# An encoder trunk on one core: sixteen more chunks of the MLP's activated branch computed with tokens on partitions, and the MLP ordered in groups of 512 columns

## The chip, the core and the metric

The kernel runs on one core of a Trainium2 chip. A core has a matrix engine (TensorE, PE in the profile, with its weight loads as PEld), VectorE (DVE), ScalarE (ACT), GpSimd (POOL) and SyncE (SP), which here issues nearly all DMA transfers. Each engine works through its own queue in order, and engines wait for each other by semaphores. The metric is the device time of one execution in microseconds (us); smaller is better.

## What is computed

Two layers (DEPTH = 2) on 256 tokens of width 1024, all in float32. In each layer a token mixer (pooling, windowed attention, gates) and then a gated MLP with a convolution over tokens on one branch:

```python
def _conv_ffn(xn, w_up, conv_w, conv_b, w_down):
    a, gval = jnp.split(xn @ w_up, 2, axis=-1)
    a = lax.conv_general_dilated(a, conv_w[:, None, :], window_strides=(1,),
                                 padding=((CONV_WIDTH // 2, CONV_WIDTH // 2),), ...)  + conv_b
    return (jax.nn.gelu(a) * gval) @ w_down

def reference(...):
    h = x
    for layer in range(DEPTH):
        h = h + _token_mixer(_rmsnorm(h, norm1[layer]), ...)
        h = h + _conv_ffn(_rmsnorm(h, norm2[layer]), ...)
    return _rmsnorm(h, norm_f)
```

The MLP's inner width D_FF is 2816: 22 chunks of 128 channels. `a` is called the activated branch here and `gval` the gate branch. The convolution has three taps over neighbouring tokens, for each channel by itself.

## The kernel before

**Precision by splitting.** Every float32 operand of a large product is split into a high part in a reduced format that TensorE takes at full pace (`wh`, made by a cast on ScalarE, line 201) and the rest (`wl`, a subtraction on VectorE, line 203). A product is high x high + high x low + low x high. The activations (`x2`, the chunks `act`) are split in the same way.

**Weights** (class `Weights`, line 97). All loads and pieces are listed in order of use (`W.use`, lines 303 to 322 for the MLP). A load is 1 MB, in one of RAW = 3 buffers, and is split as two pieces of 128 x 1024; BUFS = 5 split pieces are held, and `get` (line 224) splits up to LOOK = 3 pieces ahead of the one that is used. Three hooks tie the order: `queue_behind` (line 152) puts the next splits behind given instructions on ScalarE and VectorE, `loads_behind` (lines 135, 722) puts a load behind another DMA in SyncE's queue, and `after_splits` (line 230) puts an instruction behind the latest splits. A scheduler then fixes the order of instructions on each engine when the program is built; nothing is reordered between engines' queues later.

**Two ways to compute a piece of the up projection.**
- `proj` (line 551) with channels on partitions: the weights are the stationary operand. A chunk of 128 channels takes 8 matmuls of 512 columns (high weights against high and low x of 256 tokens) and 8 of 256 columns (low weights against high x). The two sums are added by ScalarE and VectorE (`add_up`, lines 579 and 580).
- `by_tokens` (line 672) with tokens on partitions: x is the stationary operand and 512 columns of weights stream (`v_sum`, line 661). Four chunks take 2 x 4 x 6 = 48 matmuls of 512 columns. The result has to be turned into channels on partitions: `cross` (line 704) does a 32 x 32 block transposition on VectorE (line 711), a write to DRAM (line 713) and four reads from it (line 718), 0.5 MB each way. `by_halves` (line 1245) does a group of four chunks in two halves.

**The MLP before** (lines 1208 to 1333). The gate branch of chunks 0 to 19 is made by tokens, in NQ = 5 groups of four; the activated branch by tokens for chunks 0 to 3 alone, and by `proj`, two chunks at a time, for 4 to 21. `up(f)` (line 1261) finishes a chunk: scaled copy with bias on ScalarE (line 1273), the other two taps on VectorE (lines 1274 and 1277), gelu on ScalarE (1286), the product with the gate branch on VectorE (1288, or 1294 for chunks 20 and 21), then the split into `actq` (ScalarE, 1297) and `actk` (VectorE, 1298). `down` is a generator over the chunks of the down projection (`residual_mm`, line 589): 12 matmuls of 512 columns a chunk (lines 585 to 587); the last four chunks are held and added quarter by quarter of the output (two token halves x two column halves), so that the norm that follows (`Norm.add`, line 441, `to_channels`, line 463) begins while later quarters are still summed. Two chunks are made, and the down projection follows LAG = 6 chunks behind; `HALF_GROUPS` says where the halves of gate groups 3 and 4 stand between them.

**The start of the MLP.** `to_channels` turns the normed tokens to channels: TensorE transposes (line 481), ScalarE makes the high part of `x2` (line 484) and VectorE the low part (line 485), for one half of the tokens (t = 0) and then the other. Behind t = 1, `queue_behind` puts the next six splits behind these parts (lines 489 and 490). The first matmuls by tokens on the new x stand in line 667.

## Time and profile before

| what | value |
|---|---|
| median of 3 runs | 862.62 us (862.19 to 862.68) |
| profiled execution | 862.26 us |
| its span, first to last instruction | 860.5 us |
| granted TensorE clock, mean | 0.999 |
| matmuls | 4343 |
| DMA moved | 186.80 MB, mean 217 GB/s |

The span is what the trace covers; the time of the execution has 1.8 us more around it. Busy times of the engines overlap, so their sum means nothing; an engine's idle time costs only where the chain of work that ended last passes through it. A matmul's end in the trace is modelled: in a stream of matmuls the next one starts before the shown end of the last, so lengths of a stretch are taken from start to start. ScalarE's and VectorE's instructions overlap a little in the same way when they follow each other without a wait.

### The profile page before, as it was taken

The numbers are of one execution on the slowest core, as the hardware profiler recorded it, in microseconds if no ns is written. First come the engines' busy times: TensorE is split into PE (matmuls) and PEld (weight loads), VectorE is DVE, ScalarE is ACT, GpSimd is POOL, SyncE is SP. The second block draws the span as 40 slices with busy tenths as digits, with TensorE's granted clock in tenths as the row PEclk, the third lists the DMA queues.
The fourth block names the chain that finished last, engine by engine and source line by source line (L and its number), as shares of the span: only waits on it lengthen the run. The fifth ranks groups of instructions, "written<-read, shape, count | busy, mean of one in ns | idle before, by whom it ended". The sixth has DMA issues, their size and how long they took to land.

```text
span 860.5 us, 11694 instructions
## 1 busy us (share of the span) xinstructions
PE 852.6 (99%) x4343; PEld 728.3 (85%) x4343; DVE 618.8 (72%) x946; ACT 492.8 (57%) x770; POOL 32.7 (4%) x98
## 2 busy tenths in 40 slices
PE   9999999999999999999999999999999999999997
PEld 8888888888888888888888889888888888888886
DVE  7998786557766787777755987764666766876774
ACT  7656665555445566566545666664554555755662
POOL 1800000000010000000000000000000100000001
PEclk9999999999999999999999999999999999999999
DMA  9686556776747786566626565657876387775741
GB/s 335 210 254 200 196 177 227 240 265 197 256 157 247 269 276 236 196 237 203 244 98 200 187 202 195 207 182 250 274 238 246 131 274 237 267 256 182 243 147 49
DMA packets 136384, 186.80 MB, mean 217 GB/s; under 512 B 5560, under 2 KB 88192, under 8 KB 136328
## 3 DMA queue, kind: packets, MB, share of 16 engines
q1 hardware_dynamic: 136168, 185.79, 64.4%
q8 instruction: 34, 0.56, 0.3%
q10 hardware_dynamic: 160, 0.27, 0.1%
q14 instruction: 22, 0.18, 0.1%
HBM read 172.39 MB, written 13.65 MB: 216 GB/s over the span
## 4 chain that ended last, share of the span: by engine, by line
PE 95%; DVE 2%; ACT 1%; issue 1%; DMA 1%; POOL 0%; POOLq 0%; ACTq 0%
PE proj_ps L543 33%; PE t_ps L667 30%; PE v_ps L667 6%; PE res_ps L587 5%; PE res_ps L585 5%; PE res_ps L586 5%; PE v_ps L895 3%; PE v_ps L802 1%; PE pool_ps L543 1%; PE o_ps L1083 1%; PE s_ps L1034 1%; PE s_ps L1029 1%; PE o_ps L1079 1%; DVE h L445 1%; DMA raw<-in_w_in_dram 1%
## 5 line engine op out<-in xcount | busy, mean ns | idle before, releaser
L203 DVE TENSOR_TENSOR wl<-raw,wh 128x1024 fp32r<-128x1024 f32 x274 | 331.9, 1220 | 134.8 <-ACT wh L201 109.0
L201 ACT CAST wh<-raw 128x1024 fp32r<-128x1024 f32 x274 | 284.9, 1050 | 132.4 <-PE t_ps L667 64.7
L543 PE MATMUL proj_ps<-x,wh 128*128 128x512 f32 x832 | 196.9, 390 | 0.0
L543 PEld LDWEIGHTS proj_ps<-x,wh 128*128 128x128 f32 x832 | 154.3, 188 | 30.9
L667 PE MATMUL t_ps<-wh,x 128*128 128x512 f32 x576 | 180.1, 390 | 0.0
L667 PEld LDWEIGHTS t_ps<-wh,x 128*128 128x128 f32 x576 | 108.2, 188 | 22.4
L667 PE MATMUL t_ps<-wl,x 128*128 128x512 f32 x288 | 112.0, 389 | 0.0
L543 PEld LDWEIGHTS proj_ps<-x,wl 128*128 128x128 f32 x832 | 105.4, 191 | 3.0
L543 PE MATMUL proj_ps<-x,wl 128*128 128x256 f32 x832 | 107.8, 283 | 0.0
L586 PE MATMUL res_ps<-wl,actq 128*128 128x512 f32 (+1 forms) x184 | 69.9, 380 | 0.0
L587 PE MATMUL res_ps<-wh,actk 128*128 128x512 f32 (+1 forms) x184 | 69.9, 380 | 0.0
L585 PE MATMUL res_ps<-wh,actq 128*128 128x512 f32 (+1 forms) x184 | 69.7, 381 | 0.0
L667 PEld LDWEIGHTS t_ps<-wl,x 128*128 128x128 f32 x288 | 54.1, 188 | 11.1
L667 PE MATMUL t_ps<-wh,po 128*128 128x512 f32 x128 | 41.4, 395 | 0.0
L587 PEld LDWEIGHTS res_ps<-wh,actk 128*128 128x128 f32 x184 | 34.6, 188 | 6.6
L586 PEld LDWEIGHTS res_ps<-wl,actq 128*128 128x128 f32 x184 | 34.6, 188 | 6.4
L585 PEld LDWEIGHTS res_ps<-wh,actq 128*128 128x128 f32 x184 | 34.5, 188 | 6.3
L579 ACT COPY a<-proj_ps 128x256 f32<-128x256 f32 x36 | 13.8, 388 | 37.4 <-PE proj_ps L543 37.4
L580 DVE TENSOR_TENSOR a<-proj_ps,a 128x256 f32<-128x256 f32 x36 | 15.0, 423 | 24.5 <-ACT a L579 24.4
L454 POOL TENSOR_SCALAR ss<-ss 128x1 f32<-128x1 f32 x8 | 1.9, 236 | 781.8 <-ACT junk L447 781.8
L667 PEld LDWEIGHTS t_ps<-wh,po 128*128 128x128 f32 x128 | 24.0, 188 | 4.9
L447 ACT ACTIVATE junk<-h 128x512 f32<-128x512 f32 (+1 forms) x19 | 10.5, 554 | 29.6 <-DVE h L445 29.5
(204 smaller groups left out, 1101.0 us busy)
## 6 DMA issues: line engine op xcount, KB each, us to landing
raw<-in_w_in_dram SPq DMA_DIRECT2D x58, 1024.0 KB, 5.8
raw<-in_w_up_dram SPq DMA_DIRECT2D x44, 1024.0 KB, 6.1
raw<-in_w_down_dram SPq DMA_DIRECT2D x22, 1024.0 KB, 4.9
raw<-in_w_a_dram SPq DMA_DIRECT2D x8, 1024.0 KB
raw<-in_w_o_dram SPq DMA_DIRECT2D x8, 1024.0 KB, 7.1
crossing<-crossing SPq DMA_DIRECT2D x12, 512.0 KB, 5.1
turning<-turning SPq DMA_DIRECT2D x8, 512.0 KB, 2.7
turned_p<-turning SPq DMA_DIRECT2D x32, 128.0 KB, 3.3
```

Of the source, the lines that this page charges most:

```text
L201: inst = nc.scalar.copy(out=h, in_=src)
L203: inst = nc.vector.tensor_sub(out=l, in0=src, in1=h.bitcast(F32))
L445: nc.vector.tensor_add(out=h[:, t, cc], in0=ps, in1=h[:, t, cc])
L447: nc.scalar.activation(junk[:, 0 : cc.stop - cc.start], h[:, t, cc], AF.Square, scale=D**-0.5, accum_out=ss[:, n : n + 1],)
L543: nc.tensor.matmul(out, w(k), x, start=(steps is first and k == 0), stop=(steps is last and k == nk - 1), skip_group_check=turns["rest"],)
L579: nc.scalar.copy(out=out, in_=sums[1])
L580: nc.vector.tensor_add(out=out, in0=sums[0], in1=out)
L585: nc.tensor.matmul(ps, ah, wh, start=first, stop=False, skip_group_check=on)
L586: nc.tensor.matmul(ps, ah, wl, start=False, stop=False, skip_group_check=on)
L587: nc.tensor.matmul(ps, al, wh, start=False, stop=last, skip_group_check=on)
L667: nc.tensor.matmul(ps, x2[:, 2 * n + j, part, t, :], w[:, j, :], start=(n + m == 0), stop=(n == last and m == 5),)
L895: nc.tensor.matmul(ps[t], a[:, k, t, :], w[:, j, :], start=(k + m == 0), stop=(k == KD - 1 and m == 2),)
```

## The change

The activated branch of chunks 4 to 19 is made by tokens too, in groups of four, so that only chunks 20 and 21 are left to `proj`. The order is now a list of steps: the activated half (`a`), the gate half (`g`) and the four chunks of the down projection (`d`) of the group before; at the end chunks 20 and 21 by `proj` (`p`) and the down projection of chunks 16 to 21. `CHUNKS_BEHIND` says which chunks `up` finishes behind which half step. Each group has its own half of two buffers for the turned results. In `to_channels`, the next two splits are also put behind the low part of x of token half 0.

```diff
-LAG = 6
-HALF_GROUPS = {4: (3, 0), 8: (3, 1), 12: (4, 0), 14: (4, 1)}
+def _mlp_steps():
+    steps = []
+    for n in range(1, NQ):
+        steps += [("a", n), ("g", n), ("d", 4 * n - 4)]
+    last = 4 * NQ
+    steps.append(("p", last))
+    return steps + [("d", f) for f in (last - 4, last)]
+MLP_STEPS = _mlp_steps()
+CHUNKS_BEHIND = {
+    ("a", 1): ((), (0, 1)), ("g", 1): ((2, 3), ()),
+    **{("d", 4 * n): ((), (4 * n + 4,)) for n in range(NQ - 1)},
+    **{("a", n): ((4 * n - 3,), (4 * n - 2,)) for n in range(2, NQ)},
+    **{("g", n): ((4 * n - 1,), ()) for n in range(2, NQ)},
+    ("p", 4 * NQ): ((4 * NQ - 3, 4 * NQ - 2), (4 * NQ - 1,)),
+}
...
-            if t == 1:
-                W.queue_behind(last, 6)
+            W.queue_behind(last if t else last[1:], 6 if t else 2)
...
-        z_of = [zg[:, 0], zg[:, 1], zga[:, 0]]
-        za = zga[:, 1]
+        z_of = {(kind, n): z[:, n % 2] for kind, z in (("g", zg), ("a", zga)) for n in range(NQ)}
...
-            if f < 4:
+            if f < 4 * NQ:
                 nc.scalar.copy(
-                    out=a.rearrange("p (a j t) -> p t a j", t=2, j=32), in_=of_chunk(za, f)
+                    out=a.rearrange("p (a j t) -> p t a j", t=2, j=32),
+                    in_=of_chunk(z_of["a", f // 4], f % 4),
                 )
             else:
                 sums = proj(x2, 2)
...
+        def half_steps(kind, n):
+            if kind == "p":
+                for f in (n, n + 1):
+                    up(f)
+                    yield
+            elif kind == "d":
+                for _ in range(n, min(n + 4, NF), 2):
+                    next(down)
+                    next(down)
+                    yield
+            else:
+                yield from by_halves(kind, n)
+        for at in MLP_STEPS:
+            if at[0] == "d" and at[1] == 4 * NQ:
+                break
+            chunks = CHUNKS_BEHIND.get(at, ((), ()))
+            for _, some in zip(half_steps(*at), chunks):
+                for f in some:
+                    up(f)
```

The list of loads (lines 303 to 322) follows the same steps: two loads for each `a` and each `g` (512 rows x 512 columns each), two for each `d` of four chunks, and two of 256 columns for `p`.

More of the change, by code (lines that the diff above doesn't have):

```diff
@@ L306, in encoder @@
             W.use(rows(w_up[l], j * 512, 4, 0, 512, tag), slots[2 * j : 2 * j + 2])
-        for n in range(3):
-            for j in range(2):
-                W.use(rows(w_up[l], j * 512, 4, DFF + n * 512, 512))
-        for f in range(4, NF, 2):
-            if f in HALF_GROUPS:
-                n, j = HALF_GROUPS[f]
-                W.use(rows(w_up[l], j * 512, 4, DFF + n * 512, 512))
-            a = cols(w_up[l], f * P)
-            if f >= 4 * NQ:
-                g = cols(w_up[l], DFF + f * P)
-                a = [a[0], g[0], a[1], g[1]]
-            W.use(a)
-            if f >= LAG:
-                W.use(rows(w_down[l], (f - LAG) * P))
-        for f in range(NF - LAG, NF, 2):
-            W.use(rows(w_down[l], f * P))
+        for j in range(2):
+            W.use(rows(w_up[l], j * 512, 4, DFF, 512))
+        for kind, n in MLP_STEPS:
+            if kind == "p":
+                (a0, a1), (g0, g1) = (cols(w_up[l], c + n * P) for c in (0, DFF))
+                W.use([a0, g0, a1, g1])
+            elif kind == "d":
+                for f in range(n, min(n + 4, NF), 2):
+                    W.use(rows(w_down[l], f * P))
+            else:
+                for j in range(2):
+                    W.use(rows(w_up[l], j * 512, 4, (kind == "g") * DFF + n * 512, 512))
     h = const.tile([P, 2, D], F32, name="h")
@@ L1243, in of_chunk, with by_halves @@
             return z[:, :, i].rearrange("p (t a) j -> p t a j", t=2)
-        def by_halves(n):
+        def by_halves(kind, n):
             ps = by_tokens(x2, 4, end=2)
@@ L1248, in by_halves @@
             by_tokens(x2, 4, ps=ps, begin=2)
-            to_z(ps, z_of[n % 3], 0, W.last[1])
+            to_z(ps, z_of[kind, n], 0, W.last[1])
             yield
@@ L1257, in encoder @@
             W.free(i)
-        to_z((ps0, ps1), za, 2, W.behind[1])
-        run(by_halves(0))
+        to_z((ps0, ps1), z_of["a", 0], 2, W.behind[1])
+        run(by_halves("g", 0))
         def up(f):
@@ L1290, in up @@
                     in0=y2.rearrange("p (a j t) -> p t a j", t=2, j=32),
-                    in1=of_chunk(z_of[f // 4 % 3], f % 4),
+                    in1=of_chunk(z_of["g", f // 4], f % 4),
                 )
@@ L1315, in encoder @@
         )
-        for n in (1, 2):
-            for j, _ in enumerate(by_halves(n)):
-                up(2 * (n - 1) + j)
-        groups = {n: by_halves(n) for n in range(3, NQ)}
-        for f in range(4, NF, 2):
-            if f in HALF_GROUPS:
-                next(groups[HALF_GROUPS[f][0]])
-            up(f)
-            up(f + 1)
-            if f >= LAG:
-                next(down)
-                next(down)
+        def half_steps(kind, n):
+            if kind == "p":
+                for f in (n, n + 1):
+                    up(f)
+                    yield
+            elif kind == "d":
+                for _ in range(n, min(n + 4, NF), 2):
+                    next(down)
+                    next(down)
+                    yield
+            else:
+                yield from by_halves(kind, n)
[6 more added lines that the diff above has]
+                    up(f)
         if l + 1 < DEPTH:
```

## The prediction

> **What bounds the kernel now.** I read the page first (span, busy shares, chain), then TensorE's timeline through the MLP, then the timelines of the other engines where the MLP ends, then the DMA issues. From the page:

> ```profile
> span 860.5 us, 11694 instructions
> ...
> PE 852.6 (99%) x4343; PEld 728.3 (85%) x4343; DVE 618.8 (72%) x946; ACT 492.8 (57%) x770; POOL 32.7 (4%) x98
> ...
> PE 95%; DVE 2%; ACT 1%; issue 1%; DMA 1%; POOL 0%; POOLq 0%; ACTq 0%
> ```

> TensorE is busy all the time and makes 95% of the chain that ends last. So nothing on another engine is worth anything here except where it makes TensorE wait, and a change can gain only by cheaper matmuls or by removing one of the few waits. It can lose wherever VectorE (72%) or ScalarE (57%) falls behind for a stretch.

> **The matmuls.** These rows of TensorE's timeline (start, length, line, operation, tiles, shape, count) hold two pairs of chunks by `proj`, 24 matmuls of the down projection, and half a group by tokens:

> ```profile
> 331.01 2.08 PE L543 MATMUL proj_ps<-x,wl 128*128 128x256 f32 x16
> ...
> 332.92 3.82 PE L543 MATMUL proj_ps<-x,wh 128*128 128x512 f32 x16
> ...
> 336.58 0.39 PE L585 MATMUL res_ps<-wh,actq 128*128 128x512 f32 x1
> ...
> 342.02 0.39 PE L667 MATMUL t_ps<-wh,x 128*128 128x512 f32 x1
> ...
> 347.46 3.79 PE L543 MATMUL proj_ps<-x,wh 128*128 128x512 f32 x16
> ...
> 351.08 2.08 PE L543 MATMUL proj_ps<-x,wl 128*128 128x256 f32 x16
> ...
> 353.00 0.40 PE L585 MATMUL res_ps<-wh,actq 128*128 128x512 f32 x1
> ```

> A pair by `proj` took 336.58 - 331.01 = 5.57 us, then 353.00 - 347.46 = 5.54. By tokens the same two chunks are 24 matmuls of 512 columns: 347.46 - 342.02 = 5.44. Both ways stream as many columns; by tokens saves the surplus of the 16 narrow ones, which start 0.12 us apart instead of half of 0.227. The change moves 8 pairs in each of 2 layers: 16 x 0.115 = **1.85 us gained**.

> [...]

> **The x parts.** The other edit puts the next two splits behind the low part of x for token half 0. Before (a group row, then the timeline of VectorE and TensorE at the first layer's start of the MLP):

> ```profile
> L667 PE MATMUL v_ps<-v,x 128*128 128x512 f32 x24 | 7.1, 416 | 0.8 <-DVE x L485 0.8
> ```

> ```profile
> 246.55 1.22 DVE L203 TENSOR_TENSOR wl<-raw,wh 128x1024 fp32r<-128x1024 f32 x1
> ...
> 247.33 0.71 PE L667 MATMUL v_ps<-v,x 128*128 128x512 f32 x2
> ...
> 247.69 0.69 DVE L485 TENSOR_TENSOR x<-xt_ps,x 128x512 fp32r<-128x512 f32 x1
> ...
> 248.43 1.20 PE L667 MATMUL v_ps<-v,x 128*128 128x512 f32 x4 [0.39 <-DVE x L485]
> ```

> A weight's low part (1.22 us) stands ahead of x's, and TensorE waits; the group row holds both layers' waits, 0.8. Since a matmul in a stream starts 0.39 - 0.227 = 0.16 before the modelled end of the last, each costs 0.55: **1.1 us gained**. In the order as built, x's low part now stands ahead of that split, which can start at about 249 and is wanted after 252, so nothing replaces the wait.

> **Work of the other engines.** Per moved chunk VectorE loses an add and gets half a transpose:

> ```profile
> L580 DVE TENSOR_TENSOR a<-proj_ps,a 128x256 f32<-128x256 f32 x36 | 15.0, 423 | 24.5 <-ACT a L579 24.4
> L711 DVE STREAM_TRANSPOSE crossing<-t_ps 128x512 f32<-128x512 f32 x20 | 13.4, 701 | 3.9 <-PE t_ps L667 3.9
> ```

> 32 x 0.423 = 13.5 us go, 16 x 0.701 = 11.2 come; ScalarE copies from SBUF where it copied from PSUM. Hidden under TensorE either way: nothing, until VectorE is what TensorE waits for.

> **A group in the middle.** One cycle (4 activated, 4 gate, 4 down pieces) is 12 x 2.72 = 32.6 us of TensorE; VectorE needs 12 x 1.14 for low parts, 4 x 0.70 for transposes, 4 x 1.46 for chunks: 22.3 us. The chunks of a group are made some 15 us after its gate half and wanted after 32.6. The first weight load behind the crossing is the tightest:

> ```profile
> 293.70 0.37 SPq L713 DMA_DIRECT2D crossing<-crossing  x1
> ...
> 299.93 1.81 SPq L718 DMA_DIRECT2D zga<-crossing  x4
> 301.84 0.94 SPq L137 DMA_DIRECT2D raw<-in_w_up_dram  x2
> ```

> ```profile
> raw<-in_w_in_dram SPq DMA_DIRECT2D x58, 1024.0 KB, 5.8
> raw<-in_w_up_dram SPq DMA_DIRECT2D x44, 1024.0 KB, 6.1
> ```

> SyncE's queue holds the load until the crossing's write has landed and the four reads are issued: 8.1 us, after 1.3 of transposes; 6.1 to land, 2.1 to split: 17.6 us after the gate half. TensorE wants it 8 pieces, 21.8 us, after. 4 us of cover: cost 0. The down projection's loads now come in fours behind a group's gate half instead of in ones; they are as many, and 8 of the 22 loads of w_up in each layer change from runs of 256 columns to runs of 512. I cost that at nothing for the same cover; if it is gone, it is the rival of late crossings.

> **The end of each MLP** is where I expect the loss. Before:

> ```profile
> 396.93 3.79 PE L543 MATMUL proj_ps<-x,wh 128*128 128x512 f32 x16
> ...
> 404.38 3.82 PE L543 MATMUL proj_ps<-x,wh 128*128 128x512 f32 x16
> ...
> 408.04 0.39 PE L585 MATMUL res_ps<-wh,actq 128*128 128x512 f32 x1
> ```

> ```profile
> 403.25 0.42 DVE L580 TENSOR_TENSOR g<-proj_ps,g 128x256 f32<-128x256 f32 x1
> ...
> 413.19 0.42 DVE L1298 TENSOR_TENSOR actk<-g,actq 128x256 fp32r<-128x256 f32 x1
> ```

> The last pairs (chunks 20, 21) take 408.04 - 396.93 = 11.1 us; VectorE starts on their sums 6.3 us after the start and has the last low part at 413.6, with four down pieces (10.9 us) still between 408.04 and the chunks that are held. No wait. After the change only chunks 16 and 17 (5.44 us) lie between, and chunks 17, 18, 19 are made in the same stretch as 20 and 21. In the order as built, VectorE's first sum of the pair (it waits for TensorE, 6.1 us after the pair's start) has 31 instructions behind it up to the low part of chunk 19: in all 7 low parts of weights, 10 passes of the convolution, 15 of 256 columns. Back to back they take less than their length:

> ```profile
> 288.95 3.50 DVE L203 TENSOR_TENSOR wl<-raw,wh 128x1024 fp32r<-128x1024 f32 x3 [0.53 <-ACT wh L201]
> ...
> 283.63 0.87 DVE L1274 SCALAR_TENSOR_TENSOR y<-a,prm,y 128x255 f32<-128x255 f32 x2
> ...
> 285.21 0.75 DVE L1288 TENSOR_TENSOR g<-y,zg 128x256 f32<-128x256 f32 x2
> ```

> ```profile
> 287.88 3.90 ACT L201 CAST wh<-raw 128x1024 fp32r<-128x1024 f32 x4
> ...
> 269.86 1.08 ACT L1273 ACTIVATE y<-a,prm 128x256 f32<-128x256 f32 x2
> ```

> Spacings: (3.50 - 1.22)/2 = 1.14, 0.39, 0.33. So 7 x 1.14 + 10 x 0.39 + 15 x 0.33 = 16.9 us; the low part of 19 is there at 6.1 + 16.9 = 23.0 at best. TensorE gets to it at 11.1 + 5.44 + 2.40 (chunk 18: nine wide, three narrow) + 0.68 = 19.6. **At least 3.4 us of waiting**, in pieces: for chunk 17, for 18, most for 19, behind which chunks 20 and 21 stand although they are ready. Walked out with ScalarE's spacings (casts 0.95, scaled copies 0.5, the small ones 0.3), its queue adds 0.8: 4.2. In layer 0 the cast of the next layer's third load stands ahead of chunk 19's cast on ScalarE. Its buffer comes free with the fifth low part, by the walk 16.8 us after the pair's start; it lands 5.8 later and is cast by 23.6, and chunk 19's high part is there at 24.1, against 11.1 + 5.44 + 2.40 = 18.9 on TensorE without any wait: **5.2 us** in all. In layer 1 no next weights are split, but TensorE's first matmul of the quarter behind chunk 18 waits for an add that is the 31st instruction of the same count (6 + 10 + 15: 15.7 us, so at best 21.8; TensorE is there at 11.1 + 5.44 + 9 x 0.227 = 18.6): bound 3.2, walked **4.1 us**. The norm behind layer 0 has its own short wait either way: 0, between -0.5 and +0.6.

> **Sum**, against the profiled execution (862.26; its span 860.5 and 1.8 around it; 0.36 under the median of 862.62): 862.26 - 1.85 - 1.1 + 5.2 + 4.1 = **868.6 us**. With the bounds (3.4 and 3.2) 865.9; with loads a microsecond or two later at both ends, 871.

> **Rivals.**
> *Cover holds.* VectorE keeps up and only the gains are left: 862.26 - 2.95 = 859.3, faster. It speaks for it that its average is 72% and that it stands idle for some 6 us just before the pair's sum; against it that the sum is ahead in its queue, so the idle time can't be used. It decides if 16.9 us of work shrank below 13.5. Half-way it would be no change. 8 in 100 (5 faster, 3 same).
> *The clock drops after the wait.* The start of the kernel shows a slow pace:

> ```profile
> 0.76 2.90 PE L372 MATMUL gain_ps<-const-float32-1.0 128*128 128x128 f32 x12 [0.76 <-PEq L1346]
> ...
> 252.19 0.60 PE L481 MATMUL xt_ps<-ident,xn 128*128 128x128 f32 x4
> ```

> ```profile
> 0.00:2.00 2.00, 1.24 (x6) 1.27 (x7) 0.19 (x5) 0.66 (x1) 0.69 (x6) 1.00 0.07 17
> ```

> 128 columns: 0.22 us apart at first, 0.11 later, though the granted clock reads 1.00 in both. If a wait of 3 to 4 us brought that back for as long as at the start (to about 5 us), each layer would lose 2.4: 873.4. Against it: no wait in this trace is longer than 0.5, so nothing shows it. 10 in 100. [...]
> *Crossings late.* 8 more of 1 MB (written and read); loads queue behind them. If the 4 us of cover are overdrawn by 1 us at each of 8 groups: 876. Against: 17.6 of 21.8 us. 7 in 100.
> *x's wait stays* (the edit doesn't do what it says): 869.7. 5 in 100.

> **How the numbers follow.** Forecast 70 in 100, its own range 865.9 to 871. Range 865.0 to 873.5: forecast, clock, x's wait, 85 in 100. Faster by over 0.2% (1.7 us, about what can be told from no change): 0.05; within: 0.03; slower: 0.92.

> **What would show it.** Right: TensorE idle 3 to 5 us in the down projection of chunks 17 to 19 in both layers, released by ScalarE or VectorE; no idle there in the middle groups; no wait on x at the first matmuls; 24 t_ps matmuls in 5.44 us. Wrong: no gap behind the last pairs, matmuls spaced wider after it (clock), or ScalarE waiting for loads with TensorE behind it in the middle groups.

## The result and the profile after

The changed kernel takes 869.88 us, the median of five runs (867.71 to 872.57). The kernel before takes 862.41 (862.01 to 862.68). The ratio is 1.0089, with a 95% interval of 1.0072 to 1.0106: the change costs 7.5 us. The forecast was 868.6, in a range of 865.0 to 873.5.

The changed kernel's runs lie 4.9 us apart, those of the kernel before 0.7. The profile below shows a cause of the wider spread. Late runs occur without the change too: beside the first four experiments the kernel before ran 22 times, 19 times in 861.83 to 863.93 us and three times in 865.15 to 868.11, and what made those three late is not shown. The run that was profiled is the longest of the five, 872.57 us with a span of 870.8.

The page of the changed kernel, with the same three rows as before:

```profile
span 870.8 us, 11486 instructions
...
PE 856.6 (98%) x4215; PEld 724.2 (83%) x4215; DVE 619.9 (71%) x930; ACT 492.3 (57%) x770; POOL 34.5 (4%) x98
...
PE 91%; DVE 3%; DMA 3%; ACT 2%; issue 1%; SPq 0%; POOL 0%; POOLq 0%; ACTq 0%
```

The chain that ends last is no longer TensorE's nearly alone: VectorE, ScalarE and a DMA hold 8% of it, against 4%. TensorE has 128 matmuls fewer (16 pairs, 32 against 24), yet its busy time grew by 4.0 us. Both need an explanation, the waits and the longer matmuls. The waits of TensorE by releaser (total us, times, longest):

```profile
PE res_ps L598 <- ACT actq L1310: 4.4, 5, 3.1
PE res_ps L598 <- DVE res_ps L633: 2.6, 1, 2.6
...
PE xt_ps L495 <- DVE xn L486: 0.2, 1, 0.2
```

The waits on x are gone from this list. The two new rows are both in the down projection (`res_ps`), where the forecast put them. TensorE's timeline in layer 0 behind the last pair, which began at 401.08:

```profile
415.44 0.50 PE L598 MATMUL res_ps<-wh,actq 128*128 128x512 f32 x1 [0.34 <-ACT actq L1310]
...
418.81 0.50 PE L598 MATMUL res_ps<-wh,actq 128*128 128x512 f32 x1 [0.30 <-ACT actq L1310]
...
424.59 0.50 PE L598 MATMUL res_ps<-wh,actq 128*128 128x512 f32 x1 [3.06 <-ACT actq L1310]
...
426.31 0.63 PE L599 MATMUL res_ps<-wl,actq 128*128 128x512 f32 x1
426.73 0.63 PE L600 MATMUL res_ps<-wh,actk 128*128 128x512 f32 x1
427.16 0.63 PE L598 MATMUL res_ps<-wh,actq 128*128 128x512 f32 x1
```

TensorE waits a little for chunk 17, a little for 18 and 3.06 us for 19; start to start the three cost 0.16 more each, 4.2 us, and with small losses in the same stretch 4.5. Then the matmuls are 0.427 us apart (426.31, 426.73, 427.16), not 0.227. The same stretch and that of layer 1 by windows of about 3.4 us (window, its length, busy TensorE and matmuls, granted clock, DMA share, GB/s; the row of 1.90 us is the idle time ahead of the first):

```profile
421.60:425.10 3.50, 0.51 (x2) 1.00 0.54 152
425.10:428.60 3.50, 3.50 (x10) 0.53 1.00 321
428.60:432.00 3.40, 3.40 (x16) 0.98 1.02 391
```

```profile
850.00:851.90 1.90, 0.00 (x0) 1.00 0.00 0
851.90:855.30 3.40, 2.73 (x7) 0.51 0.00 0
855.30:858.70 3.40, 3.40 (x9) 0.50 0.00 0
858.70:862.10 3.40, 3.40 (x17) 0.99 0.00 0
```

The granted clock falls to 0.50 for one such window in layer 0 and for two in layer 1, and the pace halves with it. In layer 0 that costs about half of 3.5 us, 1.7; in layer 1 half of the 6.1 us from 852.57 to 858.70, 3.0. In the profiled run the pace thus costs 4.7 us on top of the waits. The five runs fit this: the mean granted clock was 0.998 in the run of 867.71 us, 0.997 and 0.996 in those of 869.88 and 869.42, and 0.993 in those of 871.77 and 872.57. One window at half clock is worth 0.002 of that mean (half of 3.41 us in a span of 870.8). It is a rough sign, because it also counts the time behind the last matmul, where the clock falls again and slows nothing (at 869.04 us in the profiled run; the kernel before, whose one fall comes at 859.59, behind its last matmul, reads 0.999).

So the span's growth of 10.3 us comes out of these parts: -1.7 to -1.85 matmuls, -1.1 waits on x, -0.6 at the meeting of the layers, +4.5 and +4.1 waits at the two ends of the MLP, +1.7 and +3.0 half pace, and 0.3 more between the last matmul and the end.

### The profile page after: what moved, and what is told of

Same layout as the page of the kernel before. It is cut to its first block, busy times and chain, and to the rows that moved or that the text cites. A ratio compares the mean times of both kernels' runs of the same rounds, so it can differ in the third digit from the quotient of the medians.

```text
span 870.8 us, 11486 instructions
## 1 busy us (share of the span) xinstructions
PE 856.6 (98%) x4215; PEld 724.2 (83%) x4215; DVE 619.9 (71%) x930; ACT 492.3 (57%) x770; POOL 34.5 (4%) x98
## 4 chain that ended last, share of the span: by engine, by line
PE 91%; DVE 3%; DMA 3%; ACT 2%; issue 1%; SPq 0%; POOL 0%; POOLq 0%; ACTq 0%
PE t_ps L680 38%; PE proj_ps L556 22%; PE v_ps L680 6%; PE res_ps L598 5%; PE res_ps L600 5%; PE res_ps L599 5%; PE v_ps L908 3%; DVE wl L221 2%; PE v_ps L815 1%; PE pool_ps L556 1%; DMA crossing<-crossing 1%; PE o_ps L1096 1%; PE s_ps L1047 1%; DMA raw<-in_w_up_dram 1%; PE s_ps L1042 1%; PE o_ps L1092 1%
## 5 line engine op out<-in xcount | busy, mean ns | idle before, releaser
L680 PE MATMUL t_ps<-wh,x 128*128 128x512 f32 x832 | 259.0, 390 | 0.0
L680 PEld LDWEIGHTS t_ps<-wh,x 128*128 128x128 f32 x832 | 156.2, 188 | 32.3
L680 PE MATMUL t_ps<-wl,x 128*128 128x512 f32 x416 | 161.9, 389 | 0.1
L556 PE MATMUL proj_ps<-x,wh 128*128 128x512 f32 x576 | 136.5, 390 | 0.0
L556 PEld LDWEIGHTS proj_ps<-x,wh 128*128 128x128 f32 x576 | 106.6, 188 | 21.2
L680 PEld LDWEIGHTS t_ps<-wl,x 128*128 128x128 f32 x416 | 78.1, 188 | 16.7 <-DVE wl L221 0.5
L556 PE MATMUL proj_ps<-x,wl 128*128 128x256 f32 x576 | 74.9, 283 | 0.0
L556 PEld LDWEIGHTS proj_ps<-x,wl 128*128 128x128 f32 x576 | 72.8, 191 | 1.9
L724 DVE STREAM_TRANSPOSE crossing<-t_ps 128x512 f32<-128x512 f32 x36 | 24.4, 701 | 9.8 <-PE t_ps L680 9.8
L1287 DVE SCALAR_TENSOR_TENSOR y<-a,prm,y 128x255 f32<-128x255 f32 x44 | 20.6, 477 | 11.0 <-ACT y L1286 11.0
## 6 DMA issues: line engine op xcount, KB each, us to landing
raw<-in_w_in_dram SPq DMA_DIRECT2D x58, 1024.0 KB, 5.8
raw<-in_w_up_dram SPq DMA_DIRECT2D x44, 1024.0 KB, 5.3
raw<-in_w_down_dram SPq DMA_DIRECT2D x22, 1024.0 KB, 5.3
raw<-in_w_a_dram SPq DMA_DIRECT2D x8, 1024.0 KB, 6.1
raw<-in_w_o_dram SPq DMA_DIRECT2D x8, 1024.0 KB, 4.7
```

The source lines that it names most:

```text
L556: nc.tensor.matmul(out, w(k), x, start=(steps is first and k == 0), stop=(steps is last and k == nk - 1), skip_group_check=turns["rest"],)
L680: nc.tensor.matmul(ps, x2[:, 2 * n + j, part, t, :], w[:, j, :], start=(n + m == 0), stop=(n == last and m == 5),)
L724: nc.vector.transpose(out=y[:, t].rearrange("p q c j -> p c q j"), in_=rows[t])
L1287: nc.vector.scalar_tensor_tensor(out=y[:, 1:], in0=a[:, : S - 1], scalar=w0, in1=y[:, 1:], op0=ALU.mult, op1=ALU.add)
```

## The experiments

Theory: the loss comes only from the end of each MLP, where VectorE's queue (and in layer 0 a load behind it) delivers chunk 19 late, and from TensorE's half pace that the idle time brings. Rivals: the loss is spread over the crossings and regrouped loads; the half pace has another cause; the line of the norm is worth something else than the two waits. Each kernel was timed beside the kernel before, whose medians were 862.66 (experiments 1 to 4), 862.41 (5 to 7), 861.96 (8, 9) and 862.61 (10, 11).

### 1. The norm's line alone

This is the kernel before with one line of the change:

```diff
-            if t == 1:
-                W.queue_behind(last, 6)
+            W.queue_behind(last if t else last[1:], 6 if t else 2)
```

> The kernel before with only the new line of the norm's end: the next two splits are queued behind the low part of x for token half 0. Theory: the two waits of TensorE on that low part (0.55 us each at the two starts of the MLP) go and nothing takes their place: 862.4 - 1.1 = 861.3 us. Rival: the split that now comes later is wanted at once, and TensorE waits for it instead: 862.4.

Measured: 859.66 us (859.59 to 860.18), ratio 0.9965 (0.9953 to 0.9977): 3.0 us gained and not 1.1 (2.7 between the spans of the profiled runs, 860.5 and 857.8). All that the waits view still lists for TensorE stands at the kernel's start:

```profile
PE gain_ps L372 <- PEq L1345: 0.8, 1, 0.8
PE v_ps L801 <- DVE m L219: 0.2, 1, 0.2
```

What the theory missed stands where the layers meet. TensorE's timeline there, first of the kernel before, then of this one:

```profile
428.39 0.28 PE L587 MATMUL res_ps<-wh,actk 128*128 128x256 f32 x1
428.77 0.41 PE L481 MATMUL xt_ps<-ident,xn 128*128 128x128 f32 x2
429.68 0.44 PE L481 MATMUL xt_ps<-ident,xn 128*128 128x128 f32 x2 [0.49 <-DVE xn L472]
```

```profile
427.42 0.29 PE L586 MATMUL res_ps<-wh,actk 128*128 128x256 f32 x1
427.54 0.60 PE L481 MATMUL xt_ps<-ident,xn 128*128 128x128 f32 x4
427.89 0.36 PE L584 MATMUL res_ps<-wh,actq 128*128 128x256 f32 x1
```

Before, the four transposes of the norm behind layer 0 came in two halves with 0.9 us lost beside them; now they run through. The same norm code ends there, so the line reorders VectorE at this place too: in the kernel before the low part of a weight (1.23 us at 424.47) stands ahead of the sums that make `xn`, here such a low part comes behind them, at 431.26. Twice 0.55 and 0.9 are 2.0 of the 2.7 between the spans; of the other 0.7, 0.3 is there already ahead of the first place that the line touches (the first transposes of the norm stand at 244.8 instead of 245.1), and 0.4 stays open.

### 2. The last pair earlier

```diff
-    steps.append(("p", last))
+    steps.insert(-1, ("p", last))
...
+    ("p", 4 * NQ): ((4 * NQ - 4, 4 * NQ - 3), (4 * NQ - 2,)),
+    ("d", 4 * NQ - 8): ((4 * NQ - 1,), ()),
```

> The changed kernel with the last pair of chunks (20 and 21) ahead of the down projection of chunks 12 to 15 instead of behind it, and chunks 16 to 19 made in the pair's stretch and in the first half of that down projection. Theory (the loss is only the backlog of VectorE and ScalarE at the end of each MLP, and the slow pace of TensorE that follows the wait): with 16.3 us of down projection instead of 5.4 between the pair and chunk 18 both waits go and with them the slow pace; what is left are the gains: 862.4 - 1.85 - 1.1 - 0.6 (the shorter wait where the layers meet) = 858.9 us, up to 860. Rival 1: the backlog only moves, and the down projection of chunks 13 to 16 waits 3 to 4 us in each layer: 866 and more. Rival 2: the loss is spread over the groups (crossings ahead of loads): most of it stays, 867 and more.

Measured: 861.97 us (860.84 to 863.97), ratio 0.9992 (0.9984 to 1.0001). The long waits for chunk 19 and the half pace are gone, 7.9 us against the changed kernel, but 3 us of the expected gain did not come. Its waits:

```profile
PE xt_ps L496 <- DVE xn L487: 1.7, 1, 1.7
PE res_ps L600 <- DVE wl L222: 1.2, 2, 0.6
```

Four chunks by tokens and the pair are now made in one stretch; the low part of a weight stands behind some of them on VectorE and comes 0.5 to 0.6 us late, once in each layer, and where the layers meet `xn` is 1.7 us late. That is a weak form of rival 1 (0.7 to 0.8 us a layer from start to start, not 3 to 4); rival 2 is out.

### 3. The long wait filled

```diff
                 for j, (i, part) in enumerate(held):
+                    if filler and t == m == 0 and j == 1:
+                        idle_ps = mmp.tile([P, 512], F32, tag="mm", name="idle_ps")
+                        ah, _, wh, _ = held[0][1]
+                        for _ in range(filler):
+                            nc.tensor.matmul(idle_ps, ah[:, 0], wh[:, 0, 0:512], start=True, stop=True)
 ...
```

> The changed kernel with ten more matmuls of 512 columns (2.3 us) in each layer, of chunk 18 into a PSUM tile that nobody reads, ahead of the matmuls of chunk 19, so that TensorE is busy in most of the long wait. Work is added, none left out. Theory (TensorE's half pace behind the wait comes from its idling): the waits keep their ends, 424.6 and 852.6 us, the idle parts of them shrink from 3.1 and 2.6 us to under 1, the matmuls behind them are 0.227 us apart from the first on, and 1.7 + 3.0 us go: 872.5 - 4.7 = 867.8 us in every run. Rival (the half pace has another cause, such as the loads of that moment): the matmuls behind the wait are still 0.427 apart, 870 to 873, or slower by the added matmuls.

Measured: 867.71 us (867.19 to 868.36), ratio 1.0057 (1.0045 to 1.0069): twenty more matmuls, 2.2 us less, and the runs 1.2 us apart instead of 4.9. TensorE's timeline in layer 1:

```profile
847.99 2.43 PE L651 MATMUL idle_ps<-wh,actq 128*128 128x512 f32 x10
850.89 0.50 PE L598 MATMUL res_ps<-wh,actq 128*128 128x512 f32 x1 [0.47 <-ACT actq L1315]
851.23 0.40 PE L599 MATMUL res_ps<-wl,actq 128*128 128x512 f32 x1
...
851.70 0.39 PE L598 MATMUL res_ps<-wh,actq 128*128 128x512 f32 x1
```

The wait ends no earlier on the other engines' account (in layer 0 at 424.48 against 424.59; in layer 1 at 850.89 against 852.57, but there everything stands the 1.7 us earlier that layer 0 no longer loses). The matmuls behind it start 0.34 us apart once, as behind the short waits, and then 0.23 to 0.24. It is the idle time that brings the half pace, and 867.7 us is what the changed kernel costs without it.

### 4. Less work for VectorE

```diff
+            if f not in (17, 18, 19):
                 nc.vector.scalar_tensor_tensor(
                     out=y[:, 1:], in0=a[:, : S - 1], scalar=w0, in1=y[:, 1:], op0=ALU.mult, op1=ALU.add
                 )
...
```

> The changed kernel without the two convolution passes on VectorE for chunks 17, 18 and 19 (six instructions in each layer, 0.39 us apart, 2.35 us): part of the computation is left out. Theory (VectorE's backlog makes the waits, in layer 0 by way of the buffer that a low part frees for the next layer's load): in layer 1 the waits shrink from 4.1 to about 1.8 us, in layer 0 from 4.5 to about 3, by the passes that stand ahead of that low part; without the slow pace 867.8 - 3.8 = 864.0 us, with it up to 868. Rival (ScalarE's queue or the landing of loads by itself sets the end): the waits stay within 0.5 us, 867.5 to 872.

The kernel leaves out two of the three taps of the convolution for chunks 17 to 19. Measured: 865.05 us (863.75 to 869.39), ratio 1.0022 (1.0004 to 1.0041). Its waits:

```profile
PE res_ps L598 <- ACT actq L1311: 2.3, 2, 1.5
PE xt_ps L495 <- DVE xn L486: 2.1, 1, 2.1
```

At the ends of the MLP 2.3 us of waiting are left of 7.0: 1.5 in layer 0 and 0.8 in layer 1, even less than expected. VectorE's backlog makes them. Part of what was gained in layer 0 comes back as 2.1 us where the layers meet, and behind that wait the clock fell again (window, length, busy TensorE and matmuls, clock):

```profile
427.80:431.20 3.40, 1.30 (x12) 1.00 1.00 384
431.20:434.60 3.40, 3.40 (x18) 0.52 0.06 20
```

### 5. Three groups of the four

```diff
+NA = 4
...
+    for f in range(4 * NA, NF, 2):
+        steps += [("p", f), ("e", f - 6)]
+    return steps + [("e", f) for f in range(NF - 6, NF, 2)]
...
-            if f < 4 * NQ:
+            if f < 4 * NA:
                 nc.scalar.copy(
```

(`e` is a `d` of two chunks; `NA` is the number of groups with the activated branch by tokens, group 0 among them.)

> The changed kernel with the activated branch by tokens for chunks 0 to 15 alone (12 of the 16 chunks of the change); chunks 16 to 21 go by pairs as before, and the down projection runs six chunks behind, so that four of its pieces (10.9 us) lie between the last pair and the held chunks, as in the kernel before. Theory (each moved pair gains 0.115 us, and the loss comes only from the end of the MLP): no wait at the end, and 859.7 (the kernel before with the norm's line alone) - 12 x 0.115 = 858.3 us. Rival 1: groups of crossings and grouped down projections cost of themselves: 859.7 or more. Rival 2: the backlog now sits at chunks 13 to 15: 861 and more.

Measured: 858.42 us (857.79 to 858.76), ratio 0.9949 (0.9936 to 0.9961): the fastest kernel of the study, 4.0 us under the kernel before. The only wait of TensorE that its waits view lists is that of the kernel's first instructions:

```profile
PE gain_ps L393 <- PEq L1374: 0.8, 1, 0.8
```

Against experiment 1, twelve pairs moved in all gave 1.4 us by the ratios (0.9965 and 0.9949, whose intervals overlap), 1.0 by the medians (4.0 and 3.0 gained) and 0.9 by the spans (857.8 and 856.9): 0.08 to 0.115 us each. The crossings and the grouped down projections cost at most 0.5 us in all.

### 6. Filled, without the norm's line

Experiment 3 with that line taken back:

```diff
-            W.queue_behind(last if t else last[1:], 6 if t else 2)
+            if t == 1:
+                W.queue_behind(last, 6)
```

> The changed kernel with the ten filling matmuls of the third experiment, and with the norm's line as it was before the change (the splits not queued behind x for token half 0). Theory (the line takes away the two waits of 0.55 us at the starts of the MLP and part of the one where the layers meet, here 0 to 0.6): 867.7 + 1.1 to 1.7 = 868.8 to 869.4 us. Rival 1 (the line is worth all of the 2.8 us that it gave alone): 870.5. Rival 2 (the regrouped loads would have removed the waits anyway): 867.7.

Measured: 869.41 us (868.80 to 869.55), ratio 1.0077 (1.0063 to 1.0091), 1.7 us above experiment 3. The waits on x are back, and the one on `xn` is 0.2 us longer than in experiment 3:

```profile
PE v_ps L686 <- DVE x L499: 0.8, 2, 0.4
...
PE xt_ps L495 <- DVE xn L486: 0.3, 1, 0.3
```

The line is worth 1.7 us in the changed kernel (1.3 by these waits) and 3.0 in the kernel before: where the layers meet, TensorE waits here with the line as well.

### 7. The pair between two halves

```diff
-    steps.insert(-1, ("p", last))
+    steps[-1:] = [("e", last - 8), ("p", last), ("e", last - 6)]
...
+    ("p", 4 * NQ): ((4 * NQ - 4,), (4 * NQ - 3,)),
+    ("e", 4 * NQ - 6): ((4 * NQ - 2, 4 * NQ - 1), ()),
```

> The changed kernel with the last pair between the two halves of the down projection of chunks 12 to 15, chunks 16 and 17 made in the pair's stretch and 18 and 19 behind the first two pieces that follow it: four pieces (10.9 us) lie between the pair and chunk 18, and the chunks are not made in one bunch, as they were in the second experiment, where low parts of weights came late. Theory (the bunch is what delays VectorE): no wait over 0.3 us in the down projection, 859.7 - 16 x 0.115 = 857.9 us, with a late load where the layers meet up to 859.5. Rival (any place of the pair leaves VectorE late with four chunks fewer ahead): waits of 1 us or more before chunks 16 to 19 in both layers, 861 and more.

Measured: 865.23 us (864.48 to 867.30), ratio 1.0030 (1.0018 to 1.0042). The theory failed and the rival holds:

```profile
PE res_ps L599 <- ACT actq L1311: 4.6, 4, 1.7
...
PE res_ps L601 <- DVE actk L1312: 0.6, 2, 0.3
```

Smaller bunches do not help by themselves. With four pieces behind the pair, TensorE gets to chunk 16 and then 18 before VectorE does, in both layers.

### 8 and 10. Chunk 19 ahead of the next layer's load

Both are experiment 3 with one more edit. In 8 it stands behind the loop over the steps, in 10 right behind chunk 19, as here:

```diff
+                    if f == 4 * NQ - 1 and l + 1 < DEPTH:
+                        W.queue_behind(made, 2, starts[l + 1] + 2)
```

> The third experiment (the changed kernel with ten filling matmuls) with one more edit: in layer 0 the splits of the next layer's third load are queued behind the high and low part of chunk 19 on ScalarE and VectorE. In the third experiment ScalarE waits for that load with chunk 19 behind it. Theory (the prediction's step: the load sets the last 0.6 to 1 us of the wait in layer 0): TensorE gets chunk 19 at about 423.8 us instead of 424.5, 867.7 - 0.6 = 867.1 us. Rival (VectorE's product is the last thing in any case): 424.5 and 867.7 again.

Measured: 867.38 us (867.00 to 867.66), ratio 1.0058 (1.0045 to 1.0071). ScalarE's order had not changed:

```profile
422.90 1.05 ACT L219 CAST ybig<-raw 128x1024 fp32r<-128x1024 f32 x1 [0.70 <-DMA raw<-in_w_in_dram]
423.86 0.40 ACT L1317 CAST actq<-g 128x256 fp32r<-128x256 f32 x1
```

The splits were traced before the line could take hold of them. This run is a repeat of experiment 3 and tells nothing about the load.

> The eighth experiment again, with its edit placed so that the order on ScalarE really changes (in the eighth the cast of the next layer's third load still stood ahead of chunk 19's): now chunk 19's high part stands ahead of that cast in layer 0. Theory (the load sets the last part of the wait in layer 0): VectorE's product for chunk 19 ends at about 423.4, the cast follows, TensorE starts at 423.8 instead of 424.3 to 424.5: 0.5 to 0.7 us off 867.4 to 867.7, so 866.7 to 867.2 us. Rival (VectorE's product is the last thing in any case): no change, 867.4 to 867.7.

Measured: 867.70 us (866.92 to 868.00), ratio 1.0053 (1.0040 to 1.0066). Now the order is the other one (ScalarE, then TensorE's wait where the layers meet):

```profile
422.65 0.41 ACT L1317 CAST actq<-g 128x256 fp32r<-128x256 f32 x1 [1.13 <-DVE g L1307]
422.97 1.05 ACT L219 CAST ybig<-raw 128x1024 fp32r<-128x1024 f32 x1
```

```profile
PE xt_ps L496 <- DVE xn L487: 0.6, 1, 0.6
```

Chunk 19's high part starts 1.2 us earlier, but 0.7 of that belongs to the whole execution, not to the edit: TensorE gets to chunk 17 at 414.62 here and at 415.30 in experiment 8, and the norm's first transposes already stand at 244.66 and 245.34. The other 0.5 is the edit's: TensorE's idle time ahead of chunk 19 goes from 0.69 us in experiment 8 to 0.16. The load did set the last part of the wait. The time does not follow: about 0.45 us comes back where the layers meet (in the list of experiment 3 that wait is too short to appear), and the median is that of experiment 3.

### 9 and 11. The down projection later

```diff
-    steps.append(("p", last))
+    steps[-4:] = [("a", NQ - 1), ("g", NQ - 1), ("d", last - 12), ("p", last), ("d", last - 8)]
...
+    ("d", 4 * NQ - 12): ((4 * NQ - 5,), ()),
+    ("p", 4 * NQ): ((4 * NQ - 4,), (4 * NQ - 3,)),
+    ("d", 4 * NQ - 8): ((4 * NQ - 2,), (4 * NQ - 1,)),
```

> The changed kernel with all 16 chunks by tokens, and the end of the MLP put in another order: the last group's two branches come before the down projection of chunks 8 to 11, the last pair behind that, then the down projections of 12 to 15 and 16 and 17; chunks 16 to 19 are made in the pair's stretch and in the down projection behind it, one in each half step. Against the second experiment 10.9 us of down projection come between the last crossing and the pair, and one chunk fewer is made beside the pair. Theory (it is the amount of VectorE's work between the pair's first sum and the next low parts that decides): no wait above 0.5 us, 859.7 - 16 x 0.115 = 857.9 us, up to 858.6. Rival (with a pair by channels behind four chunks by tokens VectorE is late wherever they stand): waits of 1 us and more in both layers and where the layers meet, as in the second experiment, 861 to 862.

Measured: 859.11 us (858.81 to 861.10), ratio 0.9967 (0.9955 to 0.9979). The expected 857.9 to 858.6 was missed by 0.5 us, and the ratio is that of experiment 1 (0.9965): in this order the moved pairs show no gain over the norm's line alone that is clear of the noise. All 16 chunks go by tokens, and no wait is left in the down projection of either layer:

```profile
PE xt_ps L499 <- DVE xn L490: 0.5, 1, 0.5
```

One wait of 0.5 us (0.7 start to start) stays where the layers meet. Experiment 11 tried its likeliest cause:

```diff
+            if t == 0 and cc.stop == D and self.behind is not None:
+                W.queue_behind((sq,), 2, self.behind)
```

> The ninth experiment with one more edit: where the layers meet, ScalarE takes the sum of squares of token half 0 ahead of the cast that waits for the next layer's late load (1.8 us there). Theory (that cast in front of the sum makes the remaining wait of 0.70 us): the wait goes, 859.1 - 0.7 = 858.4 us, and all 16 chunks by tokens cost no more than their matmuls save. Rival (the low parts of the next layer's weights on VectorE, or the load itself, hold TensorE just as long): 859.1.

Measured: 859.28 us (858.80 to 859.40), ratio 0.9956 (0.9942 to 0.9971). The sum now stands ahead of the cast, and TensorE waits the same 0.5 us for `xn`; the intervals of the two ratios overlap. The late load was not it. What holds `xn` there was not settled; its multiplication waits for GpSimd's root (0.25 us of idle VectorE ahead of it), so the norm's own chain of sum, root and product is the next suspect, only argued.

## Why the forecast came out so

- **TensorE bounds the kernel**: right. Where the traces were compared, the differences come out of matmuls and of TensorE's waits and pace, but for some tenths (0.3 us at the end of the changed kernel, 0.4 open in experiment 1).
- **Matmuls, -1.85 us**: right by the rows of the changed kernel. Its last two pairs by channels take 11.13 us (401.08 to 412.21), 5.57 each; by tokens the 24 matmuls from 259.20 on start 0.227 apart, 5.45. The difference is 0.12 us; experiment 5's whole times give 0.08 to 0.115.
- **The x parts, -1.1 us**: right in the changed kernel, where both waits are gone, and mis-sized as the worth of the line: alone it gives 3.0 us. The step that failed is the sentence on the norm behind layer 0 ("its own short wait either way: 0"). That norm runs the same line, and 0.9 us of waiting went there in experiment 1; in the changed kernel 0.6 went.
- **A group in the middle, 0**: right. The group rows of the matmuls by tokens, 1248 in all, have no idle time worth naming:

```profile
L680 PE MATMUL t_ps<-wh,x 128*128 128x512 f32 x832 | 259.0, 390 | 0.0
...
L680 PE MATMUL t_ps<-wl,x 128*128 128x512 f32 x416 | 161.9, 389 | 0.1
```

- **The end of layer 0, +5.2 us**: right in place, order and cause, 0.7 too large. It measured 4.5. The walk had the third load landed at 22.6 us behind the pair's start and chunk 19's high part ready at 24.1. ScalarE's timeline, with the pair's start at 401.08:

```profile
421.93 0.42 ACT L1299 ACTIVATE y<-y 128x256 f32<-128x256 f32 x1
423.19 1.05 ACT L219 CAST ybig<-raw 128x1024 fp32r<-128x1024 f32 x1 [0.84 <-DMA raw<-in_w_in_dram]
424.14 0.40 ACT L1310 CAST actq<-g 128x256 fp32r<-128x256 f32 x1
```

  ScalarE waits for that load with chunk 19 behind it, as walked; the cast starts at 22.1 and chunk 19 is ready at 23.5.
- **The end of layer 1, +4.1 us**: right, 4.1 measured. VectorE's timeline shows the add that TensorE waits for (the last row) at the end of an unbroken queue, each row beginning before the modelled end of the one ahead:

```profile
851.41 0.43 DVE L1311 TENSOR_TENSOR actk<-g,actq 128x256 fp32r<-128x256 f32 x1
851.75 0.42 DVE L1301 TENSOR_TENSOR g<-y,zg 128x256 f32<-128x256 f32 x1
852.08 0.43 DVE L633 TENSOR_TENSOR res_ps<-res_ps,h 128x256 f32<-128x256 f32 x1
```

- **The clock, a rival of 10 in 100**: this is the part that went wrong. The forecast left it out because no wait of the kernel before, 0.5 us at most behind its start, showed it. It happened in most runs: nothing in one of the five, 1.7 to 2.2 us in two, 4.1 to 4.9 in two (each against 867.71). The rival's 2.4 us a layer are about right (1.7 and 3.0). The median lies between the forecast, 868.6, and this rival's 873.4.
- **Crossings late, x's wait stays, cover holds**: none came true.

The sizes thus made up for each other: the waits came out 0.7 us smaller than forecast, the meeting of the layers gave 0.6, and the half pace took 2.2 in the median run. The waits were foreseen by working, but that the median lies only 1.3 us from the forecast is in part luck.

## What to carry to other kernels

An engine that is 72% busy on average can still set the time: count the work that stands in its queue between the last thing that it must wait for and the first thing that the bounding engine wants from it, and compare that with the bounding engine's own work in between. Price a new wait on TensorE with what it does to the pace behind it, not by its length alone (here waits of 3.06 and 2.64 us brought 1.7 and 3.0 us of lost pace); matmuls that nobody reads can be cheaper than idling (here twenty of them took 2.2 us off the median). A change made of two edits should be taken apart: here one gives 3.0 us alone, and the other gives 1.0 to 1.4 more as soon as the last of its four groups stays as it was.

## What the runs showed of the hardware

The window ahead of a fall was not idle as a whole. Waits of 3.06, 2.64 and (experiment 4) 2.1 us brought the fall; in the 3.41 us ahead of it TensorE had been idle for 2.7, 2.0 and 2.1 us, 79, 60 and 61% of them. The waits of 1.7 us in the profiled runs of experiments 2 and 7 brought none: behind that of experiment 2 the clock reads 1.00 up to 433.0 us, and the mean of both runs is 0.999. A wait of 1.7 us is at most half of such a window, wherever it lies, but no run shows by itself that the idle share decides. In layer 1 of the changed kernel the first of the two windows at half pace still held 0.6 us of idle time, and the clock came back only behind the second, which was busy throughout. The windows do not begin with the kernel's first matmul: it starts at 0.76 us in both runs, and the first change came at 5.47 in one and at 6.26 in the other. Part of the run's start is lost with a late one: the matmuls of `v_ps` with `m` begin at 5.44 and 5.41 us, and the row of three of them with `xuh` stands at 6.59 and at 6.93. This fits that the same wait costs nothing, one window or two from run to run, but no run set the phase on purpose.

The high parts and rests took 0.227 us for 512 columns, 0.44 ns a column; the matmuls of plain float32 took 0.11 us for 128, 0.87 ns a column (four of `s_ps<-k,q` in the kernel before at 107.87 us, 0.61 long together and 0.275 each). Full pace, in the section on the kernel before, stands for the first of these two figures.
